# A hybrid S5, MLA and cross-attention layer: keys and values of the memory computed ahead of the input norm and kept in DRAM, the sine tables around a row norm, and a new step list for cross attention

## The chip, the cores and the metric

The kernel runs on one core of one Trainium2 chip. The metric is the device time of one execution in microseconds; the median of several executions is compared. Profiles and traces come from one profiled execution. TensorE's granted clock is given as a share of its 2.4 GHz, so that 0.50 is 1.2 GHz.

## The reference

One layer of depth 1 over a sequence of 1024 tokens of width 1024, and a memory of 256 tokens. All matrices are float32.

```
h  = layer_norm(x)
z  = h @ w_in                      # u (256), c_q (256), c_kv (256), k_r (32), two gates (2048)
y  = s5_ssm(u, ...)                # 16 groups, 64 states, complex diagonal recurrence
s  = gelu(y) @ w_glu               # gated by a sigmoid
q, kv from rms_norm(c_q), rms_norm(c_kv); causal attention, 8 heads, with rotary parts
m  = (sigmoid(g_s) * s + sigmoid(g_a) * a) @ w_o
x1 = layer_norm(alpha * h + m)
# cross attention: 4 heads of 256 over the memory
q  = x1 @ w_xq;  k = mem @ w_xk;  v = mem @ w_xv
x2 = layer_norm(alpha * x1 + softmax(q k^T / 16) v @ w_xo)
out = layer_norm(alpha * x2 + relu(x2 @ w_up)^2 @ w_dn)   # hidden width 4096
```

## The kernel before, in words

Every product keeps float32 accuracy by three matmuls in a rounded float32 format: each operand is split into a high part and the low rest, and `mm3` (L149 to L152) adds high x high, high x low and low x high. A weight goes through `split_w` (L109): SyncE issues its DMA into a raw buffer, ScalarE casts the high part (L120), GpSimd subtracts it to get the low part (L122). `w()` (L131) fetches weights by a list, the plan, some entries ahead of use. In the first part of the kernel the raw buffers are a pool of two ("raw"); from L1313 on they come from the large pool of thirty ("a").

The kernel is one straight program. The compiler keeps the order of each engine's instructions nearly as the scheduler leaves it, and each engine works through its own queue in that order; semaphores hold an instruction until its operands are there.

Front. SyncE loads constants, then tiles of x, then w_c and w_u. Each half of x (four tiles of 128 tokens) is normalised: statistics on VectorE, then L222 on ScalarE or L224 on VectorE in turn; `ln_T` turns it with transposes (L232), L240 to L245 write the high and low parts, and L247 spills a copy to DRAM. `c_gemm(half)` (L583) multiplies by w_c with 192 matmuls 128x512 for both halves and then makes the row norm of c_q and c_kv: squares on ScalarE (L600), mean and epsilon on VectorE (L602), reciprocal and root (L163 to L167), multiplications (L608 on VectorE, L610 on ScalarE). Between `c_gemm(0)` and `c_gemm(1)` stands the text of the S5 tables: `sincos` (L461, called for 264 columns), powers by repeated complex products (L503 to L508), coefficients (L653 to L668). Then the u product follows (L690, four blocks of 24 matmuls 128x288 while the c vectors are turned by `c_T`), then tables G and O (L714 to L728, operations of 128x1024 on VectorE), then the gate product gs.

The middle. The larger products (w_o, xq, xo, up, down) are Strassen products of seven quarter products of 48 matmuls 128x512, with sums of quarters made by L367 (copy), L371, L373 and L375 ahead, and evacuated behind. `chain` runs preparation, product and evacuation of neighbouring products staggered. The xq products (`xq_`) give the queries of cross attention. At the fifth of them `mem_T` (L1316) turns the memory with 16 transposes. Then comes a written list, `STEPS` (L1361), with one letter for each piece of work: k and v compute keys (`xk_gemm`, L1332) and values (`xv_gemm`, L1345) from the memory, s makes scores and softmax of one unit (a head and half of the tokens), t turns the probabilities, o multiplies by the values, r is one residual tile (`residual`, L271: L279, L280, L281) and c advances the chain of the xo products (`xo_`). A unit has L1378 and L1379 (split of the scaled query), 24 score matmuls 128x256, the maximum (L1394), four exponentials (L1397), the division on GpSimd (L1401), eight transposes (L1409), the casts (L1411 ScalarE, L1412 VectorE), 12 value matmuls 128x512, and copies (L1422).

Of the kernel before, what the change touches and what calls it, by code (L numbers as in the profile page):

```python
# [75 lines left out]
class K:  # L76
# [54 lines left out]
    def w(self, key, ahead=None):  # L131
# [13 lines left out]
        return self.ready.pop(key)  # L145
# [365 lines left out]
def body(tc, ctx, a, dbg=None):  # L511
# [8 lines left out]
    nc.sync.dma_start(cst, a["cst"])  # L520
    xt = a["x"].rearrange("(c s) d -> s c d", s=8)
    X = []
    for t in range(4):
        x = k_.slot("x")
        nc.sync.dma_start(x, xt[t])
        X.append(x)
# [9 lines left out]
    plan = [(("c", kp), a["w_c"][kp], 1024) for kp in range(4)]  # L536
# [6 lines left out]
    plan += [(("oa", m), a["w_oa"][m], 512) for m in range(8)]  # L543

    def acc(name, w, kps):
        return [((name, kp, nh), w[kp, nh], 1024) for nh in range(2) for kp in kps]
    plan += [None]
    xk_ = [(("xk", m), a["w_xk"][m], 1024) for m in range(8)]
    xv_ = acc("xv", a["w_xv"], range(4))
    plan += xk_[0:4] + xv_[0:4] + xk_[4:8] + xv_[4:8]  # L550
    k_.set_plan(plan)
# [7 lines left out]
    for hf in range(2):  # L559
        if hf == 1:  # L560
            X = []
            for t in range(4, 8):
                x = k_.slot("x")
                nc.sync.dma_start(x, xt[t])
                X.append(x)
        for t in range(4):
            k_.ln_tile(X[t], k_.bn_half(X[t], 1, k_.bn_half(X[t], 0)), t % 2, lt0[:, 4 * hf + t, :])
        if hf == 0:
            for kp in range(4):
                Wc.append(k_.w(("c", kp), 0))  # L570
        k_.ln_T(X, V_LNIN, lambda k: h0.get(k, hf * 512, 512),
                lambda k: d_h0[k // 2, hf, :, (k % 2) * 512:(k % 2 + 1) * 512])
    Wu = []
# [6 lines left out]
    def c_gemm(hf, fill=()):  # L580
# [23 lines left out]
        for t in ts_:  # L604
            for i in range(2):
                z = tl[t][:, i * 256:(i + 1) * 256]
                if i:
                    V.tensor_scalar(z, z, y[:, 2 * t + i:2 * t + i + 1], None, op0=ALU.mult)  # L608
                else:
                    A.mul(z, z, y[:, 2 * t + i:2 * t + i + 1])  # L610
# [36 lines left out]
    sin_t, cos_t = sc[:, 0:256], sc[:, 264:520]  # L647

# [32 lines left out]
    ct1 = c_gemm(1, [lambda k=k: c_T(0, ct0, (k,)) for k in range(4)])  # L681
# [28 lines left out]
    def bh(z):  # L710
        return z.unsqueeze(2).broadcast_to([128, 8, 8, 16])

# [15 lines left out]
    V.tensor_scalar(nci, ci, -1.0, None, op0=ALU.mult)  # L728

# [448 lines left out]
    XOO = '3657142'  # L1178
# [6 lines left out]
    XVB = 0  # L1185
# [126 lines left out]

    k_.rawtag = "a"  # L1313
    mT, xk, xv = [], [], []

    def mem_T():  # L1316
        M = [k_.slot("raw") for _ in range(2)]
        for i in range(2):
            nc.sync.dma_start(M[i], a["mem"][i * 128:(i + 1) * 128, :])
        mT.extend((k_.slot(), k_.slot()) for _ in range(2))  # L1320
        for k2 in range(4):
            b = k_.bank()
            for j in range(2):
                for i in range(2):
                    c = (2 * k2 + j) * 128
                    PE.transpose(b[:, j * 256 + i * 128:j * 256 + (i + 1) * 128], M[i][:, c:c + 128], ident)
            hi, lo = (z[:, (k2 % 2) * 512:(k2 % 2 + 1) * 512] for z in mT[k2 // 2])
            A.copy(hi.bitcast(FR), b)
            V.tensor_sub(lo.bitcast(FR), b, hi)
    mk = lambda k: tuple(z[:, (k % 4) * 256:(k % 4 + 1) * 256] for z in mT[k // 4])  # L1330

    def xk_gemm(hd):  # L1332
        if hd % 2 == 0:
            xk.append((k_.slot(), k_.slot()))
        for m in (2 * hd, 2 * hd + 1):
            W = k_.w(("xk", m))
            b = k_.bank()
            for k in range(8):
                k_.mm3(b[:, 0:256], tuple(z[:, k * 128:(k + 1) * 128] for z in W), mk(k), k == 0, k == 7)
            hi, lo = (z[:, (m % 4) * 256:(m % 4 + 1) * 256] for z in xk[m // 4])  # L1340
            A.copy(hi.bitcast(FR), b[:, 0:256])
            V.tensor_sub(lo.bitcast(FR), b[:, 0:256], hi)

    def xv_gemm(nh):
        if not xv:  # L1345
            xv.extend((k_.slot(), k_.slot()) for _ in range(2))
        bs = [k_.bank2(), k_.bank2()] if XVB else [k_.bank(), k_.bank()]
        for kp in range(4):
            W = k_.w(("xv", kp, nh))
            for i in range(2):  # L1350
                for j in range(2):
                    k = 2 * kp + j
                    k_.mm3(bs[i][:, 0:512], tuple(z[:, i * 128:(i + 1) * 128] for z in mk(k)),
                           tuple(z[:, j * 512:(j + 1) * 512] for z in W), k == 0, k == 7)
        for i in range(2):
            hi, lo = (z[:, nh * 512:(nh + 1) * 512] for z in xv[i])
            A.copy(hi.bitcast(FR), bs[i][:, 0:512])
            V.tensor_sub(lo.bitcast(FR), bs[i][:, 0:512], hi)

# [8 lines left out]
    for i in xq_:  # L1368
        if i == 5:
            mem_T()  # L1370
# [221 lines left out]
```

## Time and profile before

| quantity | value |
|---|---|
| median of 3 runs | 1651.0 us (1650.1 to 1652.37) |
| profiled execution, time | 1652.23 us |
| its span in the trace | 1650.4 us |
| TensorE busy | 1539.5 us (93%) |
| VectorE busy | 1243.3 us (75%) |
| ScalarE busy | 976.5 us (59%) |
| GpSimd busy | 988.0 us (60%) |
| mean granted TensorE clock | 0.981 |

A busy TensorE is one with a matmul running; a matmul's rate also depends on the granted clock. Time that TensorE waits is the difference between the span and its busy time. The profiled execution lies 1.83 us above its span and 1.2 us above the median.

### The profile page before, as it was taken

Reading aid. Unit: us, or ns where it says so; the run is one execution under the profiler, and the core shown is the slowest. Engines: PE = TensorE matmul, PEld = TensorE weight load, DVE = VectorE, ACT = ScalarE, POOL = GpSimd, SP = SyncE. Lnnn points to the kernel's source line nnn. Section 1 sums busy time; section 2 is a strip of 40 time slices with the busy share of each in tenths; the row PEclk is TensorE's granted clock in tenths of the full one; section 3 lists DMA queues with packets and bytes.
Section 4 is the critical chain, followed back from the end, with each engine's and each line's share of the span. In section 5 each row is a group of like instructions: output and inputs, shape, how many; then the busy total and the mean of one; then the engine's idle time right before and its main releaser. Section 6 shows DMA issues by size and latency. Waiting matters only on the chain.

```text
span 1650.4 us, 20758 instructions
## 1 busy us (share of the span) xinstructions
PE 1539.5 (93%) x7480; PEld 1263.0 (77%) x7480; DVE 1243.3 (75%) x1977; ACT 976.5 (59%) x1415; POOL 988.0 (60%) x538
## 2 busy tenths in 40 slices
PE   6979999999989999999977899899999999999995
PEld 4867778778768778778866687678888888888884
DVE  7970926767777969956574686999598949876998
ACT  5632235666678537684573647766866766667661
POOL 3223243664547767665563554676878767878776
PEclk9989999999999999999998899999999999999998
DMA  6212121111052541103220120022111302021102
GB/s 240 81 39 71 53 71 56 59 60 50 15 177 81 201 154 51 52 0 129 102 102 1 32 86 37 28 75 64 39 51 52 102 1 77 26 103 50 57 22 102
DMA packets 40107, 117.61 MB, mean 71 GB/s; under 512 B 4804, under 2 KB 6340, under 8 KB 40004
## 3 DMA queue, kind: packets, MB, share of 16 engines
q1 hardware_dynamic: 40004, 116.29, 20.5%
q8 instruction: 59, 0.97, 0.2%
q14 instruction: 44, 0.36, 0.1%
HBM read 98.90 MB, written 16.78 MB: 70 GB/s over the span
## 4 chain that ended last, share of the span: by engine, by line
PE 71%; DVE 15%; ACT 7%; POOL 3%; issue 3%; DMA 1%; SPq 0%; POOLq 0%; ACTq 0%; DVEq 0%
PE b L151 20%; PE b L150 20%; PE b L152 20%; DVE sx L1192 1%; PE bb L1034 1%; PE b L1071 1%; DVE c L182 1%; DVE t L371 1%; PE bb L1037 1%; DVE sx L1223 1%; ACT bb L367 1%; PE bb L1038 1%; PE b L1090 1%; DVE sx L224 1%; DVE sa L1249 1%
## 5 line engine op out<-in xcount | busy, mean ns | idle before, releaser
L151 PE MATMUL b<-sw,sa 128*128 128x512 f32 (+3 forms) x1504 | 579.6, 385 | 12.8 <-POOL sw L375 6.7
L150 PE MATMUL b<-sw,sa 128*128 128x512 f32 (+3 forms) x1504 | 578.6, 385 | 12.8 <-ACT sw L120 5.4
L152 PE MATMUL b<-sw,sa 128*128 128x512 f32 (+3 forms) x1504 | 577.7, 384 | 2.7 <-POOL sa L375 2.2
L151 PEld LDWEIGHTS b<-sw,sa 128*128 128x128 f32 x1504 | 284.7, 189 | 71.8 <-POOL sw L375 10.3
L150 PEld LDWEIGHTS b<-sw,sa 128*128 128x128 f32 x1504 | 284.5, 189 | 69.2 <-ACT sw L120 5.7
L152 PEld LDWEIGHTS b<-sw,sa 128*128 128x128 f32 x1504 | 284.5, 189 | 57.9 <-POOL sa L375 4.0
L375 POOL TENSOR_TENSOR sa<-t,sa 128x1024 fp32r<-128x1024 f32 x105 | 257.6, 2469 | 118.8 <-ACT sa L373 106.9
L367 ACT COPY bb<-sa 128x1024 f32<-128x1024 f32 x230 | 233.1, 1018 | 135.8 <-DVE t L371 69.1
L1192 DVE TENSOR_TENSOR sx<-sx,b 128x512 f32<-128x512 f32 x288 | 185.1, 675 | 35.2 <-PE b L152 35.0
L375 POOL TENSOR_TENSOR sw<-t,sw 128x1024 fp32r<-128x1024 f32 x73 | 180.9, 2484 | 43.4 <-ACT sw L373 34.2
L371 DVE TENSOR_TENSOR t<-bb,sa 128x1024 f32<-128x1024 f32 x119 | 144.1, 1217 | 35.1 <-ACT bb L367 18.9
L1249 DVE TENSOR_TENSOR sa<-sa,b 128x512 f32<-128x512 f32 x192 | 124.9, 678 | 46.8 <-ACT sa L1247 33.7
L373 ACT CAST sa<-t 128x1024 fp32r<-128x1024 f32 x105 | 109.1, 1049 | 59.3 <-DVE t L371 58.9
L362 POOL TENSOR_TENSOR sa<-sa,sa 128x1024 fp32r<-128x1024 f32 x36 | 90.2, 2519 | 57.8 <-ACT sa L361 34.2
L122 POOL TENSOR_TENSOR sw<-sraw,sw 128x1024 fp32r<-128x1024 f32 (+4 forms) x28 | 61.9, 2219 | 87.4 <-ACT sw L120 81.8
L150 PE MATMUL b<-sa,sw 128*128 128x512 f32 (+1 forms) x272 | 101.5, 373 | 3.3 <-DVE sa L1249 3.3
L152 PE MATMUL b<-sa,sw 128*128 128x512 f32 (+1 forms) x272 | 99.2, 365 | 0.0
L151 PE MATMUL b<-sa,sw 128*128 128x512 f32 (+1 forms) x272 | 99.2, 365 | 0.0
L362 POOL TENSOR_TENSOR sw<-sa,sw 128x1024 fp32r<-128x1024 f32 x32 | 81.1, 2550 | 27.9 <-ACT sw L361 27.9
L371 DVE TENSOR_TENSOR t<-bb,sraw 128x1024 f32<-128x1024 f32 x53 | 64.2, 1217 | 33.8 <-POOL sw L375 17.8
L373 ACT CAST sw<-t 128x1024 fp32r<-128x1024 f32 x73 | 76.2, 1052 | 15.3 <-PE b L151 7.6
L375 DVE TENSOR_TENSOR sw<-bb,sw 128x1024 fp32r<-128x1024 f32 x47 | 57.2, 1217 | 5.6 <-ACT sw L373 5.5
(341 smaller groups left out, 2792.5 us busy)
## 6 DMA issues: line engine op xcount, KB each, us to landing
sa<-in_w_up_dram SPq DMA_DIRECT2D x24, 512.0 KB, 4.0
sa<-in_w_dn_dram SPq DMA_DIRECT2D x24, 512.0 KB, 4.3
sx<-in_x_dram SPq DMA_DIRECT2D x16, 512.0 KB, 5.8
d_h<-t SPq DMA_DIRECT2D x16, 256.0 KB, 2.3
sraw<-in_w_gs_dram SPq DMA_DIRECT2D x8, 512.0 KB, 3.2
d_gs<-t SPq DMA_DIRECT2D x16, 256.0 KB, 2.9
t<-d_gs SPq DMA_DIRECT2D x16, 256.0 KB, 2.8
d_ms<-t SPq DMA_DIRECT2D x16, 256.0 KB, 2.1
```

Of the source, the lines that this page charges most:

```text
L122: (nc.vector if self.rawtag == "a" and self.nsw % SWV == 0 else nc.gpsimd).tensor_sub(lo[:, :cols].bitcast(FR), raw[:, :cols], hi[:, :cols])
L150: mm(out, A[0].bitcast(FR), B[0].bitcast(FR), start=start, stop=False)
L151: mm(out, A[0].bitcast(FR), B[1].bitcast(FR), start=False, stop=False)
L152: mm(out, A[1].bitcast(FR), B[0].bitcast(FR), start=False, stop=stop)
L182: self.nc.vector.bn_stats(st[:, h, :], x[:, h * 512:(h + 1) * 512])
L362: (GP if z is x[c] else V).tensor_sub(H[c][1].bitcast(FR), z, H[c][0])
L367: A.copy(P[c], x[c])
L371: V.tensor_tensor(T[c], P[c], y[c], op=op)
L373: A.copy(H[c][0].bitcast(FR), T[c])
L375: (V if T[c] is P[c] else GP).tensor_sub(H[c][1].bitcast(FR), T[c], H[c][0])
L1192: V.tensor_tensor(v, v, b, op=op)
L1249: V.tensor_tensor(z[:, s_], z[:, s_], b, op=op)
```

## The change

It has three parts.

First, the memory is loaded ahead of x and turned at the very beginning. The weights w_xk and w_xv become the first sixteen entries of the plan. `xk_gemm(0)` and `xk_gemm(1)` stand ahead of the first half's norm, 2 and 3 ahead of its transposes, 4 to 7 in the same way around the second half, and both `xv_gemm` follow; only then w_c is fetched and `c_gemm(0)` begins. High and low parts of keys and values are written to DRAM (`d_xk`, `d_xv`, 512 KB each, eight transfers) from SyncE's queue. In cross attention `load_kv` brings them back by eight transfers issued from GpSimd's queue, which issued none before.

Second, `c_gemm(1)` is called right behind `sincos` instead of after all the small S5 tables, and the G and O tables are held behind the last multiplication of its row norm.

Third, cross attention has a new step list without k and v, in which the first scores stand in the xq products, five of the eight residual tiles too, three r steps stay, the letter b prepares the weight side of the first two xo products early, and the xo products and the units have another order.

```diff
-    plan = [(("c", kp), a["w_c"][kp], 1024) for kp in range(4)]
+    plan = [(("xk", m), a["w_xk"][m], 1024) for m in range(8)]
+    plan += [(("xv", kp, nh), a["w_xv"][kp, nh], 1024) for nh in range(2) for kp in range(4)]
+    plan += [(("c", kp), a["w_c"][kp], 1024) for kp in range(4)]
...
-    plan += xk_[0:4] + xv_[0:4] + xk_[4:8] + xv_[4:8]
+    d_xk = k_.dr.tile([2, 2, 128, 1024], F32, name="d_xk")
+    d_xv = k_.dr.tile([2, 2, 128, 1024], F32, name="d_xv")
+    k_.w(("xk", 0), 1, False)
+    X = load_x(range(4))
...
+    def xk_gemm(m):
+        if m % 4 == 0:
+            xk.append((k_.slot(), k_.slot()))
+        W = k_.w(("xk", m))
+        b = k_.bank()
+        for k in range(8):
+            k_.mm3(b[:, 0:256], tuple(z[:, k * 128:(k + 1) * 128] for z in W), mk(k), k == 0, k == 7)
+        hi, lo = (z[:, (m % 4) * 256:(m % 4 + 1) * 256] for z in xk[m // 4])
+        A.copy(hi.bitcast(FR), b[:, 0:256])
+        V.tensor_sub(lo.bitcast(FR), b[:, 0:256], hi)
+        if m % 4 == 3:
+            for j in range(2):
+                nc.sync.dma_start(d_xk[m // 4, j], xk[m // 4][j])
...
     for hf in range(2):
+        for m in range(2):
+            xk_gemm(4 * hf + m)
         for t in range(4):
             k_.ln_tile(X[t], k_.bn_half(X[t], 1, k_.bn_half(X[t], 0)), t % 2, lt0[:, 4 * hf + t, :])
+        for m in range(2):
+            xk_gemm(4 * hf + 2 + m)
         k_.ln_T(X, V_LNIN, lambda k: h0.get(k, hf * 512, 512),
                 lambda k: d_h0[k // 2, hf, :, (k % 2) * 512:(k % 2 + 1) * 512])
+        if hf == 0:
+            X = load_x(range(4, 8))
+    xv_gemm(0)
+    xv_gemm(1)
+    for kp in range(4):
+        Wc.append(k_.w(("c", kp), 0))
...
     sin_t, cos_t = sc[:, 0:256], sc[:, 264:520]
+    ct1 = c_gemm(1, [lambda k=k: c_T(0, ct0, (k,)) for k in range(4)])
+    ct1_last = k_.last_ts.ins
...
-    ct1 = c_gemm(1, [lambda k=k: c_T(0, ct0, (k,)) for k in range(4)])
...
+    g_ = tc.issue_after(ct1_last)
...
-    XOO = '3657142'
+    XOO = '3567142'
...
-    STEPS = "k0 s0 k1 s1 t0 r0 v0 r0 t1 o0 s2 r0 k2 o1 r0 s3 t2 r0 k3 o2 r0 t3 s4 r0 o3 c0 r0 v1 t4 s5 o4 s6 c0 t5 o5 c0 t6 s7 o6 c0 t7 o7".split()
+    STEPS = "X s0 X s1 t0 V o0 s2 t1 s3 o1 r b t2 s4 o2 r t3 s5 o3 r b t4 s6 o4 t5 s7 o5 c t6 c o6 c t7 c o7 c".split()
...
+    def load_kv(key, src):
+        kv[key] = tuple(k_.slot() for _ in range(2))
+        for z, d in zip(kv[key], src):
+            nc.gpsimd.dma_start(z.bitcast(FR), d)
...
-    xu = [(hf, 2 * p + d) for p in range(2) for hf in range(2) for d in range(2)]
+    xu = [(0, 2), (0, 3), (1, 0), (1, 1), (0, 0), (0, 1), (1, 2), (1, 3)]
...
+        if z == "X":
+            p = 1 - len(kv)
+            load_kv(("k", p), [d_xk[p, j] for j in range(2)])
+        elif z == "V":
+            for i in range(2):
+                load_kv(("v", i), [d_xv[i, j] for j in range(2)])
+        elif z == "b":
+            p = early.pop(0)
+            p[0]()
+            p[1]("B")
...
+    for i in xq_:
+        if i > 1:
+            next(res)
+        if i == 4:
+            step()
+            step()
```

SyncE's queue at the start of the program before the change: constants, four x tiles (L525), two small tables, then w_c and the next x tiles in turn (a name such as `sraw30` is a raw buffer, `sx` a slot for x).

```order
L520 DMA cst_58<-in_cst_dram 128x160
L525 DMA sx1_74<-in_x_dram 128x1024
...
L533 DMA c6_84<-in_cstb_dram 128x256
L119 DMA sraw30_152<-in_w_c_dram 128x1024
L119 DMA sraw33_158<-in_w_c_dram 128x1024
L564 DMA sx56_254<-in_x_dram 128x1024
```

SyncE's queue in the changed program, a little further on: two key weights, the tiles of the second half of x, the first spills (`d_h0`), and a key weight between them.

```order
L119 DMA sraw56_270<-in_w_xk_dram 128x1024
L119 DMA sraw60_303<-in_w_xk_dram 128x1024
L530 DMA sx80_420<-in_x_dram 128x1024
...
L583 DMA d_xk_82<-sa41_155 128x1024
L247 DMA d_h0_152<-t63_341 128x512
...
L247 DMA d_h0_152<-t67_361 128x512
L119 DMA sraw86_428<-in_w_xk_dram 128x1024
L247 DMA d_h0_152<-t69_371 128x512
L119 DMA sraw90_461<-in_w_xk_dram 128x1024
```

The weight loads that stood behind four x tiles are sixteen more, and keys 6 and 7 (`sraw86`, `sraw90`) stand behind spills of the first half's transposed input.

ScalarE at the start of the changed program; `sw` are the high parts of weights, `b45` and `b49` the banks of keys 0 and 1, `c39` the statistics of the input norm.

```order
L120 CAST sw8_90<-sraw10_92 128x1024
L566 CAST sa17_106<-b22_129 128x512
L579 CAST sa40_154<-b45_162 128x256
...
L579 CAST sa40_154<-b49_195 128x256
L120 CAST sw42_156<-sraw44_158 128x1024
```

The cast of key 2's weight (`sw42`) now stands behind the copies of keys 0 and 1 out of their banks.

VectorE around the row norm of `c_gemm(1)` before the change: L602 is the mean of squares (`c126`), L163 to L167 reciprocal and root, L714 to L718 the G and O tables.

```order
L506 TENSOR_TENSOR sa108_547<-sa108_547 128x8
L602 TENSOR_SCALAR c126_828<-c126_828 128x8
L714 TENSOR_TENSOR sx154_1127<-sa108_547,sx112_554 128x1024
L163 RECIPROCAL c132_847<-c126_828 128x8
L701 COPY sx135_863<-b136_865 128x32
L716 TENSOR_TENSOR sx154_1127<-sx154_1127,sa156_1129 128x1024
L165 TENSOR_TENSOR c132_847<-c131_846 128x8
L717 TENSOR_TENSOR sx155_1128<-sa108_547,sx112_554 128x1024
```

The same place in the changed program, where the mean is L654 and the tables begin at L769.

```order
L506 TENSOR_TENSOR sa186_1021<-sa186_1021 128x8
L654 TENSOR_SCALAR c204_1261<-c204_1261 128x8
L163 RECIPROCAL c210_1280<-c204_1261 128x8
L754 COPY sx213_1337<-b214_1339 128x32
L165 TENSOR_TENSOR c210_1280<-c209_1279 128x8
...
L660 TENSOR_SCALAR sx203_1260<-sx203_1260,c209_1279 128x256 x2
L769 TENSOR_TENSOR sx232_1601<-sa186_1021,sx190_1028 128x1024
```

The operations of 128x1024 have left the norm's chain and follow its last multiplication.

ScalarE in cross attention of the changed program, from the casts of one unit's turned probabilities (L1415) to the next unit's exponentials (L1401); L1382 is the scaled query, L1426 a copy of values.

```order
L1415 CAST sa1513_8059<-b1512_8054 128x512
L1382 ACTIVATE sa1514_8062<-sa1357_7273 128x1024
L367 COPY bb1506_8034<-sa1498_8022 128x1024
L367 COPY bb1507_8036<-sa1499_8024 128x1024
L373 CAST sw1502_8030<-t1508_8038 128x1024
L373 CAST sw1504_8032<-t1509_8040 128x1024
L361 CAST sw1540_8210<-sraw1500_8026 128x1024
L361 CAST sw1542_8212<-sraw1501_8028 128x1024
L1401 ACTIVATE sa1516_8066,c1518_8080<-bb1517_8067,c1518_8080 128x256 x2
L1426 COPY sa1521_8107<-b1522_8108 128x512
```

Six preparing operations (L367, L373, L361) of the first xo products stand between two units; the casts of key and value weights (L120) that stood between the units before the change are gone from here.

## Rows read from the trace of the kernel before

**Rows 1.** The page, busy time of each engine (us, share of the span, instructions).
```profile
PE 1539.5 (93%) x7480; PEld 1263.0 (77%) x7480; DVE 1243.3 (75%) x1977; ACT 976.5 (59%) x1415; POOL 988.0 (60%) x538
```

**Rows 2.** TensorE's waits from 0 to 100 us: waited for, sum, times, longest.
```profile
PE b L232 <- DMA sraw<-in_w_c_dram: 11.3, 1, 11.3
PE b L232 <- ACT sx L610: 10.2, 1, 10.2
```

**Rows 3.** Stretches: length, busy us (instructions) of each engine, clock, DMA share, GB/s.
```profile
4.00:12.00 8.00, 0.68 (x3) 0.68 (x4) 6.46 (x21) 1.39 (x5) 0.00 (x0) 1.00 1.03 403
94.00:100.00 6.00, 5.79 (x22) 5.13 (x23) 5.28 (x9) 3.33 (x8) 0.00 (x0) 0.50 0.00 0
728.00:770.00 42.00, 42.00 (x186) 34.70 (x187) 32.43 (x38) 26.99 (x30) 28.52 (x12) 1.00 0.08 26
783.00:933.00 150.00, 122.05 (x691) 102.84 (x690) 83.97 (x112) 84.77 (x154) 74.76 (x57) 0.90 0.19 66
```

**Rows 4.** TensorE's waits from 783 to 956 us.
```profile
PE b L150 <- ACT sa L1411: 11.8, 4, 7.1
```

**Rows 5.** TensorE's timeline at several places: start, us, operation, count [idle before].
```profile
19.97 0.80 PE L150 MATMUL bb<-sw,sa 128*128 128x512 f32 x1 [0.23 <-ACT sa L244]
...
74.26 0.29 PE L150 MATMUL b<-sw,sa 128*128 128x288 f32 x1
...
783.16 0.28 PE L150 MATMUL b<-sa,sw 128*128 128x256 f32 x1
...
788.91 0.28 PE L150 MATMUL bb<-sa,sa 128*128 128x256 f32 x1
...
856.85 1.03 PE L1409 MATMUL b<-cst,sa 128*128 128x128 f32 x8
...
894.27 1.22 PE L150 MATMUL b<-sa,sa 128*128 128x512 f32 x2 [7.07 <-ACT sa L1411]
...
899.63 0.39 PE L150 MATMUL b<-sw,sa 128*128 128x512 f32 x1
...
909.84 0.39 PE L150 MATMUL b<-sw,sa 128*128 128x512 f32 x1
...
932.60 0.57 PE L150 MATMUL b<-sw,sa 128*128 128x512 f32 x1
```

**Rows 6.** Groups by line, 783 to 933 us: count, busy us, mean ns, idle before.
```profile
L122 POOL TENSOR_TENSOR sw<-sa,sw 128x1024 fp32r<-128x1024 f32 x14 | 35.7, 2569 | 12.5 <-ACT sw L120 6.4 <-PE b L152 4.0 <-PE b L151 2.1
L1397 ACT ACTIVATE sa<-bb,c 128x256 f32<-128x256 f32 x32 | 14.9, 474 | 26.5 <-DVE c L1394 26.5
L120 ACT CAST sw<-sa 128x1024 fp32r<-128x1024 f32 x13 | 13.4, 1062 | 0.0
L367 ACT COPY bb<-sa 128x1024 f32<-128x1024 f32 x11 | 11.1, 1025 | 0.7 <-DVE sx L281 0.6
L1411 ACT CAST sa<-b 128x512 fp32r<-128x512 f32 x16 | 8.9, 589 | 0.3 <-PE b L1409 0.3
L1378 ACT ACTIVATE sa<-sa 128x1024 fp32r<-128x1024 f32 x8 | 8.6, 1069 | 0.0
```

**Rows 7.** DMA issues: count, KB each, median us from issue to landing.
```profile
sraw<-in_w_gs_dram SPq DMA_DIRECT2D x8, 512.0 KB, 3.2
...
sa<-in_w_xk_dram SPq DMA_DIRECT2D x8, 512.0 KB, 5.8
```

**Rows 8.** VectorE's timeline, 78 to 96 us.
```profile
89.55 0.16 DVE L602 TENSOR_SCALAR c<-c 128x8 f32<-128x8 f32 x1
89.62 1.21 DVE L714 TENSOR_TENSOR sx<-sa,sx 128x1024 f32<-128x1024 f32 x1
```

**Rows 9.** ScalarE's timeline, 78 to 96 and 885 to 901 us.
```profile
80.17 0.40 ACT L600 ACTIVATE t<-sx 128x256 f32<-128x256 f32 x1
...
93.65 1.71 ACT L610 ACTIVATE sx<-sx,c 128x256 f32<-128x256 f32 x4 [2.15 <-DVE c L167]
...
893.63 0.58 ACT L1411 CAST sa<-b 128x512 fp32r<-128x512 f32 x1
```

## The prediction: what the change does to the time

> **What bounds the kernel now.** I read the page's busy table first: TensorE is busy for 93% of a span of 1650.4 us [rows 1], so at most some 110 us can be won without removing matmuls, and the change removes none. The question is therefore where TensorE stands still or runs at its lower clock. The TensorE waits of the first 100 us show two: 11.3 us until the first loads arrive and 10.2 us for a ScalarE operation of line 610 [rows 2]. The stretch table shows the third place: from 783 to 933 us, cross attention, TensorE is busy for 122.05 of 150 us at a mean granted clock of 0.90 [rows 3]; the longest sum of waits there is for line 1411, 11.8 us in 4 times [rows 4]. The xq stretch just ahead, 728 to 770 us, has TensorE at 42.00 of 42 with ScalarE at 26.99 and VectorE at 32.43 [rows 3]: what is put in there has room.
>
> The change touches the front and this attention; by the order of instructions the rest of TensorE's program is the same on both sides. So I work out two distances: to the end of the fourth block of the u product (100.0 us now), and from the end of the last xq product (783.2 us) to the last unit's values (932.6 us, where the next product begins) [rows 5].
>
> **Part 1, keys and values in front.** Moved work: a key weight is 24 matmuls, 48 of them take 788.91 - 783.16 = 5.75 us [rows 5], so 2.9 us each and 23 us for eight. A value weight is 12 matmuls 128x512 at (909.84 - 899.63)/45 = 0.227 us [rows 5], 2.7 us, 22 us for eight. With 2.1 us for the memory's 16 transposes (1.03 for eight [rows 5]) this is 47 us that leave the middle and stand in front.
>
> They don't simply add there, since TensorE does nothing for 11 us now and reaches its dense part at 19.97 us [rows 5]. Lower bound: memory and first weights are 2 MB after the constants, at the 403 GB/s of this stretch [rows 3] some 5.5 us after a start near 2; then ScalarE's cast of 1.06 and GpSimd's subtraction of 2.57 us [rows 6]. Key 0 is ready near 11 us. From there TensorE needs 45 us of products and 64 transposes of the input, 8.3 us; c_gemm(0) could start at about 65 to 68 us.
>
> The weights set a slower pace. A weight holds one of two raw buffers through its transfer (3.2 us for w_gs alone, 5.8 for w_xk now [rows 7]), the cast and the subtraction: 3.2 + 1.06 + 2.57 = 6.8 us, so two buffers give one in 3.4 to 3.5 us, 0.6 to 0.8 above what TensorE takes. Sixteen of them after 11 us: the first w_c is ready at about 67, and c_gemm(0), which needs all four, at about 76. The order adds holds: ScalarE's cast of key 2 is queued behind the copies of keys 0 and 1, which wait for TensorE; SyncE's loads of keys 6 and 7 and of the first values are queued behind spills of the normalised input, which wait for transposes, and behind them their own casts, 2.57 us subtractions and TensorE. These would bring the start to 84 us if none overlapped. I take 80, the middle, since some of the spills go out while TensorE is busy with keys 4 and 5.
>
> From that start to the end of the fourth u block: 192 matmuls 128x512 (two halves, eight k, four tiles, three products) at 0.227, 43.6 us; 16 transposes 2.1 and the next ones 0.5; four u blocks at 3.2 us, 12.9 (three of them stand between 74.26 [rows 5] and the 10.2 us wait, which ends at 94.2, behind line 610: 9.7). Sum 59.1. The point now reached at 100.0 is reached at 80 + 59.1 = 139.1: +39.1 us, with bounds +27 (start at 68) and +43 (start at 84).
>
> **Part 2, the row norm of c_gemm(1).** The 59.1 us already has no stall for line 610. Now VectorE gets to the squares' sums (line 602) at 89.55 and the chain goes on only behind one of the 1.21 us table operations [rows 8], while ScalarE has started the last squares at 80.17 and comes to line 610 at 93.65 [rows 9]. After the change sincos is done ahead, and no 1024-wide table operation stands inside the chain; its own work is two reductions, reciprocal, root, four multiplies of each kind: about 8 us behind the end of c_gemm(1), against 9.6 us of u blocks. The gain is 10.2 us, and 2.9 us for the slow clock right behind it: from 94 to 100 us 0.50 is granted [rows 3], half of 5.79. If VectorE were late all the same, these 13 us come back, and the sum is +3. The twelve table operations go behind the norm: 12 x 1.21 = 14.5 us of VectorE that now lie partly ahead of it; they delay only the G and O tables. The gs product lies between (eight weights of 48 matmuls at 0.227 us, 87 us), so I take nothing; without that cover it would be the 14.5 us at most.
>
> **Part 3, cross attention.** It now takes 932.6 - 783.2 = 149.4 us. In it stand 45 us of keys and values, one output product of 48 matmuls, 11.1 us, and eight units of scores (24 x 0.12 = 2.9), turns (1.03) and values (12 x 0.227 = 2.7): 53 us. That is 109 us; 40 are idle time and slow clock. After it, from the same point: seven scores (the first moves into the xq products, +3.0 us there, where the memory's transposes go, -2.2), eight turns, eight values, one output product: 20.3 + 8.2 + 21.8 + 11.1 = 61.4 us. How much idle stays? Nothing but other units can now cover the chain of a unit: scores, maximum, four exponentials at 0.474 [rows 6], division on GpSimd, turns, the two casts at 0.589, values. ScalarE's own work in a unit is 1.07 + 1.9 + 1.18 + 0.59 = 4.7 us, plus a residual copy (1.03, like line 367) in three of the units; and the early preparation for the output products puts six instructions of 1.03 us [rows 6] between two units' exponentials (lines 367, 373, 361 in the order rows). Bounds: nothing (61.4), and the longest single wait of the present, 7.1 us for line 1411 [rows 5], for each unit: 8 x 7.1 = 57 us (118). Walking the four engines' orders in step with these durations I get units of 8.5 to 12.6 us and 35 us of idle, 96.5 us in all; two of the gaps, of the 4 to 6 us size after which the clock is at 0.50 now, take 3 us more. I take 99.5: -49.9 us.
>
> K and V come back by eight transfers of 512 KB from GpSimd's queue, for which no row of before exists. Each waits for a buffer that a product of xq frees, and is wanted one 11.1 us product later or more. Bounds by the nearest rows: 3.2 and 5.8 us to land [rows 7]; four in a row at 403 GB/s are 5.2 us. Hidden at either; I take nothing. Behind them on GpSimd's queue stand subtractions for the next product, with the same slack. The Trainium skill ("SBUF — State Buffer", the "DVE blocks DMA" trap) speaks against it: a transfer issued from GpSimd has its descriptors written by GpSimd's cores, and some two-port VectorE operations lock these out of the memory meanwhile. No run here shows that yet; by the rows the sum stays, by that rule it would be rival 4's. Five residual parts now stand in xq (ScalarE 1.03, VectorE some 2.4 each, two operations of the 1.2 us of line 714 [rows 8]): 5 and 12 us, spread over five products of 11.1 us; in 42 us these engines have 15 and 10 free [rows 3], so 20 and 13 in 55: VectorE is just filled, and a product that waits a little would show here first.
>
> **Sum.** +39.1 - 49.9 + 0.8 = -10.0 us on the profiled execution's 1652.2 us, 1642.2; the median of the runs, 1651.0, lies 1.2 lower, so **1641 us**.
>
> **Rivals.**
> 1. The front gives everything back (slower). The two raw buffers don't overlap as I count: if half of the sixteen weights pay the whole 6.8 us, c_gemm(0) starts at 11 + 8 x 3.5 + 8 x 6.8 = 93 us plus the wait for the four w_c, some 97. Then the front is +56, the sum +7: 1658. It decides from a start at 90 us. For it speaks that loads, casts and subtractions stand in three in-order queues with waits of other work in them; against it that eight x tiles and the spills need only some 17 us of the transfer time, and that GpSimd and ScalarE are mostly free (casts 16 x 1.06 us).
> 2. Attention without keys and values to fill it is bound by a unit's chain: each unit waits the 7.1 us, 118 us, and the clock takes 5 more. Middle -26, sum +14: 1665. For it: that is what now happens where only units alternate. Against: in that wait ScalarE did five preparing operations of lines 367 and 373 ahead of line 1411 at 893.63 [rows 9]; in the new order only two units have such operations in between.
> 3. Everything overlaps: a start at 72 us (+31) and gaps of 3.5 us (28 us, middle 89.4, -60). Sum -28: 1623.
> 4. GpSimd's transfers are late: if the four of V take 5.8 us one after the other they need 23 us against the some 16 us they have, and the first values wait 7 us; with the same for the keys' second half +10 in all, about 1651. For it: no row shows this queue in use, and VectorE is the fullest engine beside TensorE there. Against: the slack of a whole product.
>
> **Chances.** My forecast (1634 to 1650) 0.52, rival 1 0.16, rival 2 0.09, rival 3 0.18, rival 4 0.05. A measurement can tell about 0.2% from no change, 3.3 us. Below 1647.7 lie nine tenths of my forecast's cases and all of rival 3: 0.65. Above 1654.3 lie most of rivals 1 and 2: 0.21. The rest, 0.14, is the same. The range runs from 1622 (rival 3) to 1657 (rival 1 where it begins): it leaves out the ends of rivals 1, 2 and 3, about 2 in 10.
>
> **What the profile would show.** Right: TensorE's dense work from about 11 us; c_gemm(0) at 76 to 84 us; no wait for line 660 (610 now) above 1 us; no wait for K or V tiles; 95 to 103 us from the last xq product to the last values, with waits for line 1415 (1411 now) and 1382 of 3 to 6 us. Wrong: key and value weights at more than 4.5 us apart; a wait of TensorE on a transfer; gaps in the xq products from the residual parts, or a granted clock below 0.9 in most of attention.

## The result and the profile after

The changed kernel takes 1687.7 us (median of 4 runs, 1686.73 to 1688.52) against 1651.68 us before: a ratio of 1.0219, 95% interval 1.0201 to 1.0236. It is 36 us slower, where 10 us faster were forecast. Its profiled execution has a span of 1685.6 us, 35.2 above that of before.

The page, busy time of each engine, as in [rows 1].

```profile
PE 1558.8 (92%) x7480; PEld 1277.5 (76%) x7480; DVE 1256.7 (75%) x1977; ACT 977.0 (58%) x1416; POOL 992.5 (59%) x546
```

The matmuls are as many as before, and TensorE is "busy" for 19.3 us more: it ran longer at the lower clock. The other 16 us of the span are more standing still. To find the places, the same instructions are sought in both timelines. TensorE's timeline of the changed kernel, in the columns of [rows 5]:

```profile
100.83 0.80 PE L150 MATMUL bb<-sw,sa 128*128 128x512 f32 x1 [6.59 <-DVE sa L599]
...
162.55 1.68 PE L232 MATMUL b<-cst,sx 128*128 128x128 f32 x4 [3.81 <-ACT sx L662]
...
169.12 0.38 PE L150 MATMUL b<-sw,sa 128*128 128x288 f32 x1
...
867.59 0.28 PE L150 MATMUL bb<-sa,sa 128*128 128x256 f32 x1
...
877.33 0.77 PE L150 MATMUL b<-sa,sa 128*128 128x512 f32 x1 [5.83 <-DMA sa<-d_xv]
...
967.75 0.39 PE L150 MATMUL b<-sw,sa 128*128 128x512 f32 x1
```

These are c_gemm(0) at 100.83, the row norm's wait, the first matmul behind the fourth u block and its four transposes (169.12), the end of the last xq product (867.6, was 783.2), the first matmul on the values that are loaded back from DRAM (877.33) and the end of the last unit's values (967.75, was 932.6). In the kernel before, the matmul behind the fourth u block is at 101.21, and the xq products begin with a wait that both kernels show, here before the change and then after it:

```profile
101.21 0.38 PE L150 MATMUL b<-sw,sa 128*128 128x288 f32 x1
...
725.53 0.50 PE L151 MATMUL b<-sw,sa 128*128 128x512 f32 x1 [1.25 <-POOL sw L375]
```

```profile
796.39 0.50 PE L151 MATMUL b<-sw,sa 128*128 128x512 f32 x1 [1.27 <-POOL sw L375]
```

So the front lies 67.9 us later; between it and xq 2.9 us are added; the xq products (from this wait at 725.5 and 796.4) take 71.2 instead of 57.6 us; and attention takes 100.2 instead of 149.4. 67.9 + 2.9 + 13.6 - 49.2 = 35.2 us, the whole difference.

TensorE's waits of the front, 0 to 170 us, as in [rows 2]:

```profile
PE bb L150 <- DVE sa L599: 6.6, 1, 6.6
PE bb L151 <- POOL sw L122: 5.9, 4, 1.9
PE b L564 <- DMA sx<-in_mem_dram: 5.4, 1, 5.4
PE b L152 <- POOL sw L122: 4.0, 2, 2.3
PE b L232 <- ACT sx L662: 3.8, 1, 3.8
```

The same for 796 to 968 us, as in [rows 4]:

```profile
PE b L150 <- ACT sa L1415: 15.7, 7, 4.6
PE b L151 <- POOL sw L375: 6.4, 4, 2.4
PE b L150 <- DMA sa<-d_xv: 5.8, 1, 5.8
```

Stretches of the front, columns as in [rows 3]:

```profile
20.00:40.00 20.00, 11.72 (x76) 11.01 (x76) 15.76 (x46) 12.20 (x24) 10.98 (x5) 0.77 0.69 237
70.00:101.00 31.00, 19.94 (x71) 14.76 (x72) 22.62 (x69) 8.23 (x10) 17.01 (x8) 0.89 0.39 128
101.00:110.00 9.00, 9.00 (x30) 7.17 (x31) 1.38 (x5) 1.05 (x1) 0.26 (x1) 0.72 0.78 292
```

Beside the waits of 6.6 us for line 599 and 5.4 us for the memory itself TensorE has many short ones, and the mean granted clock of these stretches is 0.72 to 0.89. Why weights come late is on ScalarE's timeline of the changed kernel, 58 to 79 us:

```profile
61.22 2.30 ACT L244 ACTIVATE sa<-b,c 128x512 fp32r<-128x512 f32 x3
65.79 0.78 ACT L244 ACTIVATE t<-b,c 128x512 f32<-128x512 f32 x1 [2.27 <-DMA d_h<-t]
66.46 1.98 ACT L120 CAST sw<-sraw 128x1024 fp32r<-128x1024 f32 x2
76.48 0.59 ACT L598 CAST sa<-bb 128x512 fp32r<-128x512 f32 x1 [8.04 <-PE bb L152]
76.97 1.05 ACT L120 CAST sw<-sraw 128x1024 fp32r<-128x1024 f32 x1
```

The casts at 66.46 are of weights whose loads had been issued at 55.2 and 58.2 us; they stand behind a turned piece of the input (line 244) that waits for a spill to leave its buffer. The cast at 76.97 stands behind a copy (line 598) that waits 8.04 us for TensorE, and TensorE needs that weight soon after. Between two casts the raw buffers are held too, so the next loads are not issued. The last value weight is ready at 91.4 us: from key 1 (14.5) on 5.5 us for each weight, not 3.5.

VectorE's timeline, 79 to 102 us, shows the 6.59 us wait:

```profile
80.46 2.36 DVE L711 TENSOR_TENSOR sa<-sa 128x8 f32<-128x8 f32 x1
...
85.02 2.24 DVE L446 TENSOR_TENSOR sa<-sa 128x8 f32<-128x8 f32 x1
...
96.23 2.26 DVE L447 TENSOR_SCALAR sa<-sa 128x8 f32<-128x8 f32 x1
...
100.09 1.28 DVE L599 TENSOR_TENSOR sa<-bb,sa 128x512 fp32r<-128x512 f32 x2
```

Line 599 is the last subtraction of the values. It frees the banks that c_gemm(0) writes, and it stands behind the exponentials of the S5 tables, a chain of tiny dependent operations. A few of these take over 2 us each; the last section comes back to them.

### The profile page after: what moved, and what is told of

Same layout as the page of the kernel before. It is cut to its first block, busy times and chain, and to the rows that moved or that the text cites. A ratio compares the mean times of both kernels' runs of the same rounds, so it can differ in the third digit from the quotient of the medians.

```text
span 1685.6 us, 20787 instructions
## 1 busy us (share of the span) xinstructions
PE 1558.8 (92%) x7480; PEld 1277.5 (76%) x7480; DVE 1256.7 (75%) x1977; ACT 977.0 (58%) x1416; POOL 992.5 (59%) x546
## 4 chain that ended last, share of the span: by engine, by line
PE 68%; DVE 14%; ACT 7%; POOL 5%; issue 4%; DMA 1%; SPq 0%; POOLq 0%; DVEq 0%; ACTq 0%
PE b L151 19%; PE b L152 19%; PE b L150 19%; DVE sx L1247 1%; PE b L1127 1%; POOL sa L375 1%; DVE t L371 1%; PE bb L1090 1%; POOL sw L375 1%; PE bb L150 1%; PE bb L151 1%; DVE sa L1304 1%; DVE sx L1278 1%; PE bb L152 1%; PE bb L1093 1%
## 5 line engine op out<-in xcount | busy, mean ns | idle before, releaser
L151 PE MATMUL b<-sw,sa 128*128 128x512 f32 (+3 forms) x1472 | 567.7, 386 | 12.0 <-POOL sw L375 11.2
L150 PE MATMUL b<-sw,sa 128*128 128x512 f32 (+3 forms) x1472 | 566.1, 386 | 10.2 <-ACT sw L361 4.4
L152 PE MATMUL b<-sw,sa 128*128 128x512 f32 (+3 forms) x1472 | 565.3, 384 | 2.7 <-POOL sa L375 2.1
L151 PEld LDWEIGHTS b<-sw,sa 128*128 128x128 f32 x1472 | 278.8, 189 | 69.5 <-POOL sw L375 15.7
L150 PEld LDWEIGHTS b<-sw,sa 128*128 128x128 f32 x1472 | 278.9, 190 | 66.1 <-ACT sw L361 4.8
L375 POOL TENSOR_TENSOR sa<-t,sa 128x1024 fp32r<-128x1024 f32 x106 | 259.8, 2468 | 115.4 <-ACT sa L373 104.8
L152 PEld LDWEIGHTS b<-sw,sa 128*128 128x128 f32 x1472 | 278.8, 189 | 57.0 <-POOL sa L375 4.0
L367 ACT COPY bb<-sa 128x1024 f32<-128x1024 f32 x230 | 233.2, 1019 | 139.5 <-DVE t L371 70.5
L122 POOL TENSOR_TENSOR sw<-sraw,sw 128x1024 fp32r<-128x1024 f32 (+4 forms) x44 | 101.0, 2305 | 121.2 <-ACT sw L120 115.6
L373 ACT CAST sa<-t 128x1024 fp32r<-128x1024 f32 x106 | 110.0, 1049 | 55.3 <-DVE t L371 54.8
L150 PE MATMUL b<-sa,sw 128*128 128x512 f32 (+1 forms) x272 | 103.4, 381 | 6.0 <-DVE sa L1304 3.3
L152 PE MATMUL b<-sa,sw 128*128 128x512 f32 (+1 forms) x272 | 101.1, 372 | 4.0 <-POOL sw L122 4.0
L151 PE MATMUL b<-sa,sw 128*128 128x512 f32 (+1 forms) x272 | 100.8, 371 | 0.0
L120 ACT CAST sw<-sraw 128x1024 fp32r<-128x1024 f32 (+4 forms) x44 | 40.5, 926 | 88.3 <-PE b L151 31.8
L371 DVE TENSOR_TENSOR t<-bb,sraw 128x1024 f32<-128x1024 f32 x53 | 64.3, 1218 | 35.2 <-POOL sw L375 17.8
L373 ACT CAST sw<-t 128x1024 fp32r<-128x1024 f32 x72 | 75.2, 1052 | 21.3 <-PE b L151 13.6
```

The source lines that it names most:

```text
L120: nc.scalar.copy(hi[:, :cols].bitcast(FR), raw[:, :cols])
L122: (nc.vector if self.rawtag == "a" and self.nsw % SWV == 0 else nc.gpsimd).tensor_sub(lo[:, :cols].bitcast(FR), raw[:, :cols], hi[:, :cols])
L150: mm(out, A[0].bitcast(FR), B[0].bitcast(FR), start=start, stop=False)
L151: mm(out, A[0].bitcast(FR), B[1].bitcast(FR), start=False, stop=False)
L152: mm(out, A[1].bitcast(FR), B[0].bitcast(FR), start=False, stop=stop)
L367: A.copy(P[c], x[c])
```

## The experiments

The ratio of each run is taken to runs of the kernel before on the same chip. These had medians of 1651.1 to 1652.7 us, so a difference from the changed kernel, whose 1687.7 us is one measurement for all, is uncertain by about 1 us.

**1. The second part alone, on the kernel before.**

```diff
     sin_t, cos_t = sc[:, 0:256], sc[:, 264:520]
+    ct1 = c_gemm(1, [lambda k=k: c_T(0, ct0, (k,)) for k in range(4)])
+    ct1_last = k_.last_ts.ins
...
+    g_ = tc.issue_after(ct1_last)      # around the G and O tables
```

> The kernel before with the second part alone: c_gemm(1) right behind sincos, the G and O tables behind its row norm. My reckoning of this part (the 10.2 us wait for line 610 and 2.9 us of slow clock behind it go): 10 to 13 us faster than before, about 1639. Rival: the changed kernel still shows a wait of 3.8 us at this place, so the chain of the norm is longer than the u blocks that cover it: 6 to 8 us faster, about 1644. If the S5 tables, now later, are waited for by something else: no gain, 1648 to 1651.

Measured: 1648.9 us, ratio 0.9977 (0.9968 to 0.9987): 3.8 us, less than the reckoning and its first rival. The number lies in the third range (1648 to 1651), but not for the reason given there: the S5 products wait 1.69 us for line 504 as before. TensorE's waits of this run, 0 to 110 us, beside [rows 2]:

```profile
PE b L232 <- ACT sx L610: 6.3, 1, 6.3
```

VectorE's timeline of this run tells why; its operations stand closely from 80 us on:

```profile
87.53 0.28 DVE L508 TENSOR_TENSOR sx<-sx 128x128 f32<-128x128 f32 x1
87.92 0.70 DVE L687 MEMSET sx<- 128x768 f32 x1
88.54 0.10 DVE L853 COPY sa<-sa 128x8 f32<-128x8 f32 x1
...
88.76 0.17 DVE L602 TENSOR_SCALAR c<-c 128x8 f32<-128x8 f32 x1
88.96 0.20 DVE L163 RECIPROCAL c<-c 128x8 f32<-128x8 f32 x1
```

Line 602 comes at 88.76, against 89.55 in [rows 8]: only the 1024-wide operations have left the chain. The small tables (lines 655 to 670, 503 to 508) still go ahead of the norm, because VectorE's order is made by readiness and they are ready earlier; the place in the text did not decide it. 4.4 us are won at the u product. At 424 to 430 us the granted clock then is 0.72, where before it was 1.00 at the same place, and of the 4.3 us that are left there 1.5 remain at 487 us. Nothing was changed in this stretch; why the clock fell there is open. The profiled execution (1650.5 us) is the slowest of the ten, so it shows more of this loss than the median.

**2. The S5 exponentials behind the values' last subtraction.**

```diff
+    s_ = tc.issue_after(k_.xv_last.ins)   # from V.tensor_copy(posf, posi) to sincos
```

> The changed kernel with the positions, exponentials and sincos of the S5 tables held on VectorE behind the last subtraction of the values. Theory: c_gemm(0) waits 6.6 us for this subtraction only because it stands behind some 50 small table operations; without them the wait and the slow clock behind it go: 6 to 10 us faster than the changed kernel, 1678 to 1682. Rival: the last two w_c loads, which stand behind the spills of the values on SyncE, become the wait in its place, or the late sincos delays c_gemm(1)'s neighbours: within 3 us of the changed kernel.

Measured: 1681.0 us, 6.7 faster than the changed kernel. c_gemm(0) starts at 95.8 with no wait for line 599 ahead of it, and the fourth u block ends 5.3 us earlier. The theory held.

**3. Raw buffers for keys and values from the large pool.**

```diff
+    k_.rawtag = "a"
     k_.w(("xk", 0), 1, False)
...
+    k_.rawtag = "raw"
     for kp in range(4):
         Wc.append(k_.w(("c", kp), 0))
```

> The changed kernel with the raw buffers of the sixteen key and value weights taken from the pool of thirty instead of the pool of two. Theory A (two buffers set the pace, each held for transfer, cast and subtraction): weights come at 2.6 to 3 us, c_gemm(0) starts 12 to 20 us earlier, 1668 to 1676. Theory B (the casts are late because they stand behind copies on ScalarE that wait for TensorE and for spills): the loads land earlier and nothing else moves, 0 to 6 us, 1682 to 1688.

Measured: 1679.5 us, 8.2 faster, between the two theories. c_gemm(0) starts at 90.3 us instead of 100.8, but it waits another 3.5 us for line 599 (600 in this run) at 95.5, and the fourth u block ends 6.0 us earlier. Keys 2 and 3 come no earlier (20.8 us, 19.5 in the changed kernel): they wait for casts behind the copies of keys 0 and 1. So buffers and the order on ScalarE share the cause, at different weights.

**4. xq products without residual tiles.** This kernel leaves the five tiles out of the computation altogether.

```diff
-    res = k_.residual(R, 1)
+    res = k_.residual(R[5:], 1)
...
-        if i > 1:
-            next(res)
```

> The changed kernel without the five residual tiles that stand in the xq products; these five tiles are left out of the computation altogether. Theory: they make VectorE late for the sums of the next product, so TensorE waits for lines 373 and 375 there: 10 to 14 us faster than the changed kernel, 1674 to 1678, and the waits of 2 us each between 833 and 855 us go. Rival: the loads on GpSimd's queue and the first scores in xq cause these waits: 0 to 4 us.

Measured: 1682.3 us, 5.4 faster. The xq products take 61.4 us instead of 71.2 (57.6 before; 58.4 with the first scores added and the memory's transposes taken out): the tiles cost 9.8 of the 12.8 us. Attention then took 104.8 instead of 100.2. TensorE's waits of this run, 796 to 968 us:

```profile
PE b L150 <- DMA sa<-d_xv: 7.2, 1, 7.2
PE b L151 <- POOL sw L375: 3.8, 3, 1.9
```

The wait for GpSimd's sums (line 375) fell from 6.4 to 3.8 us and the one for line 373 is gone; the wait for the values grew, and about half of what was won was given back in attention (2.6 us more idle, 2.0 more at the lower clock). Of the 3.8 us, 1.9 stand at the start of xq as before the change (2.0). The rest comes behind the first scores:

```profile
845.26 0.49 PE L150 MATMUL b<-sw,sa 128*128 128x512 f32 x1 [0.46 <-DVE sa L1304]
...
847.64 0.50 PE L151 MATMUL b<-sw,sa 128*128 128x512 f32 x1 [1.89 <-POOL sw L375]
```

These are 2.4 of the 3.0 us that the tiles don't explain. The sum of the second wait starts on GpSimd at 845.21, right behind the issue of two key loads that took 1.14 us there.

**5. Small S5 tables behind the norm too, on the kernel before.**

```diff
     ct1_last = k_.last_ts.ins
+    n_ = tc.issue_after(ct1_last)
...
     k_.cmul(V, bbr, bbi, frb, fib, br, bi, bt_)
+    n_.__exit__(None, None, None)
```

> The kernel before with the second part, and in addition the small S5 tables (powers and coefficients, 70 operations of 0.15 to 0.3 us) held on VectorE behind the last multiplication of the row norm, as the G and O tables are. Theory: in the second part alone the wait for line 610 only fell from 10.2 to 6.3 us because these small tables and two operations of the vectors' turn stand ahead of line 602; with them behind, the wait goes: 9 to 13 us faster than before, 1638 to 1643. Rival: the tables then are late for the S5 products, whose wait grows from 1.7 us by what was won: 1647 to 1651.

Measured: 1643.1 us, ratio 0.995 (0.9937 to 0.9964). The waits of this run, 0 to 110 us:

```profile
PE b L232 <- ACT sx L610: 2.1, 1, 2.1
```

The wait of 10.2 us is 2.1, and the S5 products wait as before (1.69 us): the tables had the time. It is faster than both kernels.

**6 and 7. The values' loads earlier, or from SyncE.**

```diff
-    STEPS = "X s0 X s1 t0 V o0 ..."
+    STEPS = "X s0 X V s1 t0 o0 ..."       # run 6
-            nc.gpsimd.dma_start(z.bitcast(FR), d)
+            nc.sync.dma_start(z, d)       # run 7
```

> The changed kernel with the V step one place earlier in the list, ahead of the second unit's scores. Theory: the first values wait 5.8 us because the four transfers stand behind that unit's divisions on GpSimd's queue; without this the wait and the slow clock behind it go: 5 to 9 us faster than the changed kernel, 1678 to 1682. Rival (GpSimd's queue itself is slow, or the buffers are not free earlier): 0 to 2 us.

> The changed kernel with the eight loads of keys and values issued from SyncE's queue instead of GpSimd's, at the same places of the list. Order theory: as the earlier V step, 5 to 9 us faster, 1678 to 1682, because SyncE has nothing in front of them. If the transfers of GpSimd's queue are slow in themselves, the earlier V step gains less than this one. Rival: the loads wait for buffers, so both leave the wait, 1685 to 1688.

Measured: 1679.9 and 1680.5 us, 7.8 and 7.2 faster; in both the wait for `d_xv` is gone. GpSimd's timeline of the changed kernel:

```profile
871.53 0.93 POOL L1405 TENSOR_SCALAR sa<-sa,c 128x256 f32<-128x256 f32 x2 [16.68 <-DVE c L1402]
872.41 0.60 POOL L1433 DMA_DIRECT2D sa<-d_xv  x1
873.05 0.93 POOL L1405 TENSOR_SCALAR sa<-sa,c 128x256 f32<-128x256 f32 x2
873.93 1.64 POOL L1433 DMA_DIRECT2D sa<-d_xv  x3
```

The first load stands behind divisions (line 1405) that wait for the second unit's sums, 16.68 us. The loads of keys and values themselves landed 3.7 to 5.9 us after issue; from SyncE's queue, in run 7, 3.3 to 7.2. It was the order, not the kind of queue.

**8. The front mended** by runs 2, 3 and the small tables of run 5 together.

> The changed kernel with three mends of the front together: exponentials and sincos behind the values' last subtraction, raw buffers of the key and value weights from the large pool, small S5 tables behind the row norm. If the two measured ones (6.7 and 8.2 us) and the third (6 us) add up: 20 us faster than the changed kernel, 1667. If the late casts on ScalarE are what all of them wait for in turn: 12 to 15 us, 1673 to 1676. In neither case is it as fast as the kernel before, so the front does not pay back.

Measured: 1668.5 us, 19.2 faster than the changed kernel, ratio to before 1.0095. The parts add up (6.7, 8.2 and the expected 6 us). c_gemm(0) starts at 89.6 us.

**9. Weights three entries ahead**, on run 8, so that the casts of keys 2 and 3 stand ahead of the copies of 0 and 1.

```diff
-    k_.w(("xk", 0), 1, False)
+    k_.ahead = 3
+    k_.w(("xk", 0), 3, False)
```

> The kernel with the mended front (1668 us) and the key and value weights fetched three entries ahead instead of two, so that on ScalarE the casts of keys 2 and 3 stand ahead of the copies of keys 0 and 1. Theory: the casts' place behind copies that wait for TensorE is what is left of the front's idle time; keys 2 and 3 start 3 to 6 us earlier and c_gemm(0) too: 1662 to 1666. Rival: the input norm and its spills (VectorE, line 245, SyncE) set the pace, so what is won at keys 2 and 3 is lost at the transposes: 1667 to 1670.

Measured: 1664.8 us, 3.7 faster than run 8 by the medians; the intervals of the two ratios (1.0062 to 1.009 here) overlap, but the trace shows c_gemm(0) 5.3 us earlier, at 84.3 us, the upper bound of the prediction. The waits at keys 2 and 3 are gone, those at the transposes between 27 and 39 us remain.

**10. All mends**: run 9, V early, and the five residual tiles as r steps in attention.

> The kernel of the run with three weights ahead, with the V step early and the five residual tiles moved from the xq products into the units of cross attention. If the parts add up (V step 7 us, xq products 10 us, less the 5 that attention took longer when they were gone): 12 us faster than the run with three weights ahead, 1651 to 1656, as fast as the kernel before and slower than the second part alone with the small tables behind. If the residual tiles cost the same in attention: 7 us, 1657 to 1661.

Measured: 1655.8 us, ratio 1.0028 (1.0015 to 1.0041). With everything repaired the kernel is 4.7 us slower than before, and 12.7 slower than run 5, which has the same norm. Against run 5 the end of the u product lies 160.5 - 106.0 = 54.5 us later, and the end of attention 936.7 - 923.2 = 13.5 later: the front costs 54.5, and what follows, the xq products and attention above all, gives back 41 for 47 us of moved work. Where the front has no room is seen from 20 to 40 us of this run, in the columns of [rows 3]:

```profile
20.00:40.00 20.00, 12.37 (x79) 10.37 (x78) 19.13 (x58) 15.03 (x30) 8.75 (x4) 0.76 0.71 256
```

VectorE, which makes the input norm here, is busy for 19.13 of 20 us, and TensorE for 12.37.

**11. The early weight sides in the old step list**, on run 5.

```diff
+        elif z == "b":
+            p = early.pop(0)
+            p[0]()
+            p[1]("B")
```

> The kernel before with the row norm mended (1643 us) and the letter b from the changed kernel at two places of the old step list (weight sides of the first two xo products made early), keys and values staying where they are. Theory: the two long waits for line 1411 (7.1 and 4.0 us) come from preparing operations on ScalarE in front of it, which are now done under the value products: 4 to 9 us faster than 1643. Rival: the same operations only wait elsewhere, ahead of lines 120 and 122: 1641 to 1646.

Measured: 1642.2 us, ratio 0.9944 (0.9931 to 0.9956), no different from run 5. The rival held; this and run 5 are the fastest versions seen.

**12. Low parts of key and value weights on VectorE**, on run 10. Three weights of w_c, fetched ahead into the same buffers, go with the sixteen.

```diff
-SWV = 100
+SWV = 1
```

> The kernel with all mends (1655.8 us), with the low parts of the sixteen key and value weights subtracted on VectorE (about 1.2 us each) instead of GpSimd (2.4). Theory: GpSimd's subtractions hold VectorE still while they run, as the tiny operations of 2.2 to 2.4 us in the changed kernel suggest, and VectorE's input norm is what the front waits for; so VectorE takes 1.2 us of work and loses up to 2.4 of waiting, and each weight is ready 1.2 us sooner: c_gemm(0) 3 to 8 us earlier, 1648 to 1653. Rival: VectorE is busy with the norm and the weights now queue behind it, 0 to 4 us slower, 1656 to 1660.

Measured: 1659.1 us, ratio 1.0039 (1.0026 to 1.0053); it is not faster than run 10, whose interval it overlaps, and c_gemm(0) starts at 88.6 instead of 84.9. The theory fell in its result. Line 245 became faster on VectorE, first run 10, then this run, 0 to 85 us:

```profile
L245 DVE TENSOR_TENSOR sa<-t,sa 128x512 fp32r<-128x512 f32 x12 | 14.6, 1226 | 4.1 <-ACT t L244 4.0
```

```profile
L245 DVE TENSOR_TENSOR sa<-t,sa 128x512 fp32r<-128x512 f32 x12 | 9.6, 821 | 0.1
```

But eighteen subtractions of 1.22 us in this stretch were more: VectorE is busy for 61.2 of its 85 us instead of 46.6.

## Why the prediction was wrong, step by step

**c_gemm(0) at 80 us: wrong by 20.8 us; this is the step that failed first.** The forecast took a weight each 3.4 to 3.5 us from two buffers, and the holds in the order as bounded by a start at 84 us, which it halved. Measured are 5.5 us for each weight, and behind the last one 6.59 us for a subtraction that stood behind S5 exponentials on VectorE. This last hold was in VectorE's order, where the forecast, which followed loads, casts and subtractions of weights, did not have it. The mends of runs 2, 3, 8 and 9 took 16.5 us of the 20.8 away by order and buffers alone (84.3).

One term of this sum was too small by itself. The forecast had 3.2 and 5.8 us for a transfer in its rows and took 3.2; in the changed kernel the page shows

```profile
sraw<-in_w_xk_dram SPq DMA_DIRECT2D x8, 512.0 KB, 5.6
...
sraw<-in_w_xv_dram SPq DMA_DIRECT2D x8, 512.0 KB, 3.9
```

With two buffers, reckoned as in the forecast, 2.4 us more for eight transfers and 0.7 for eight are 8 x 1.2 + 8 x 0.35 = 12 us. This is an estimate; run 3 takes the two buffers away, and no run takes away the longer transfers by themselves. The outcome is nearest to the first rival, whose pace was 93 - 11 = 82 us for sixteen weights, 5.2 each: c_gemm(0) came beyond its point of decision, a start at 90 us.

**59.1 us from there to the fourth u block: 68.3.** The mark itself was read 1.2 us too early: the sum ends behind the next four transposes, which in the kernel before is at 101.2 and not at 100.0, so the forecast's own +39.1 should have been +37.9. Of the 9.2 us, 2.5 were lost up to the u product, where 0.72 is granted from 101 to 110 us right behind the wait; the rest is the row norm, 3.81 us of wait and 2.9 of slow clock behind it. The step that counted some 8 us for the norm's chain, with sincos done ahead and no 1024-wide table operation inside, failed: the wide operations had gone, the small ones still stood ahead of it. Run 1 measured the part by itself at 3.8 us instead of 13; run 5, which makes the step true, at 9.5.

**xq products hide five residual tiles: they don't.** VectorE was called "just filled"; that was the place, at a price of zero. It cost 9.8 us of the 12.8 by run 4. Of the other 3.0 (the first scores' own work is counted apart) the trace of run 4 shows 2.4 as waits behind the first scores, one of them for a subtraction that stands behind two loads on GpSimd's queue; the forecast gave these subtractions "the same slack" as the loads. No run takes these waits away.

**Nothing between the u product and xq: 2.9 us.** No single wait accounts for them, and their cause is open.

**Attention 99.5 us: 100.2, right by luck, since its parts were not.** The 5.83 us wait for values was forecast as hidden. The transfer, which by the forecast is wanted one product later or more, stood behind divisions in GpSimd's order, so the fourth rival had the wait (7 us there) but not its reason: runs 6 and 7 show the order, and nothing of a lock on descriptors. Of the 38.8 us above the 61.4 of work, 25.6 are idle (35 forecast) and 13.2 slow clock (3 forecast), as this stretch of the changed kernel shows:

```profile
867.60:967.80 100.20, 74.63 (x378) 60.63 (x377) 57.80 (x83) 54.45 (x110) 37.72 (x41) 0.86 0.15 53
```

Not each wait was followed by the lower clock. Behind those of 5.83, 3.53 and 4.65 us matmuls of 512 columns follow each other at 0.43 us (shown as 0.63 us long), behind those of 1.25 and 1.12 us soon at 0.23 (0.39 us long). Two such matmuls, behind the waits of 1.25 and of 4.65 us:

```profile
890.72 0.39 PE L151 MATMUL b<-sa,sa 128*128 128x512 f32 x1
...
948.18 0.63 PE L152 MATMUL b<-sa,sa 128*128 128x512 f32 x1
```

Added up, the misses are 28.8 us in the front (67.9 for 39.1), 2.9 behind it, 12.8 in xq and 0.7 in attention: 45.2 us, the whole way from the forecast's -10.0 to the measured +35.2 of the span.

**The idea itself.** Before, keys and values filled the waits of the units. Taken out, 47 us of work gave back 41 at best (run 10). In front, TensorE stands still for 11.3 us at the start of the kernel before, and of these 5.4 us remain in the changed kernel as the wait for the memory's own load. So even with every mend the move loses 12.7 us to run 5. The forecast had the 47 us and the 11 us of free time, and bounded what attention would lose with its filler; that VectorE, with the input norm, has no room in the front (19.13 of 20 us in run 10) it did not count. That this is what holds run 10's front is read from its trace and not tested by a run; run 12, which gave VectorE more to do there, was not faster.

What stays open: how the 3.0 us in xq that run 4 leaves and the wait of 2.9 us for a transposed piece (line 240) in run 9 could go, and a wait of 1.5 us in the u product (for line 764 in run 10) that runs 8, 9, 10 and 12 show and the changed kernel does not.

## What to carry to other kernels

Work that is moved to an earlier place needs a place in every in-order queue there, not only on TensorE: follow each engine's order row by row, and ask of each cast or copy what stands ahead of it and what that waits for. Work that fills the waits of a chain costs less than its length where it stands, so taking it out gives back less: 41 us of 47 here. Where a scheduler sets the order, a call moved in the text moves nothing by itself: hold the competing operations behind the chain's last one explicitly, as run 5 does.

## What the runs showed of the hardware

A VectorE operation on 128x8 numbers, 0.15 to 0.17 us elsewhere, took 2.2 to 2.4 us five times between 80 and 99 us of the changed kernel, and each of these ends with a GpSimd subtraction. GpSimd's timeline of the changed kernel:

```profile
84.86 2.38 POOL L122 TENSOR_TENSOR sw<-sraw,sw 128x1024 fp32r<-128x1024 f32 x1 [2.07 <-ACT sw L120]
...
96.13 2.34 POOL L122 TENSOR_TENSOR sw<-sraw,sw 128x1024 fp32r<-128x1024 f32 x1 [1.79 <-ACT sw L120]
```

The subtractions end at 87.24 and 98.47; the operations of VectorE above, at 85.02 and 96.23, end at 87.26 and 98.49, and the three others in this stretch (from 80.46, 89.19 and 92.06) in the same way. The Trainium skill ("SBUF — State Buffer", section on the two separate sides) says that VectorE and GpSimd share one pair of ports as an exclusive lock for a whole instruction; the trace agrees, within 0.03 us. Run 12 agrees as well: with GpSimd nearly idle in the front, line 245 went from 1.23 to 0.82 us, and line 224 took 0.81 us twice but 1.76 and 1.51 where a GpSimd subtraction started at nearly the same time (38.26 and 46.16 us).

These holds bear on the 6.59 us wait. The five operations of 2.2 to 2.4 us and one of 1.30 at 79.17 take 12.7 us, where six of 0.17 would take 1.0. Without them, by this estimate, the chain ahead of line 599 would end some 11 us earlier, ahead of the copies of the last values (92.90 and 95.96), and the wait would hardly be there. So order and holds together made it; run 2 took away the order, and no run the holds alone.

Transfers issued from GpSimd's queue in the changed kernel landed after 3.7 to 5.9 us for 512 KB; the same queue took 0.54 to 0.75 us to issue one.
